# Where two sets of transfers stand in a decoder kernel's DMA queue, and how far ahead the sample tokens' work is woven

## The chip, the cores and the metric

The kernel runs on one core of one Trainium2 chip. The time is the device time of one execution in microseconds; the median of several executions counts. TensorE is called PE, VectorE DVE, ScalarE ACT, GpSimd POOL and SyncE SP. SP issues most direct transfers, POOL issues all indirect ones (gathers).

## The reference, cut to what matters

One layer of a decoder step works on 256 prompt tokens and on 32 sample tokens (8 sequences, 4 new tokens each). Everything is float32.

- `proj = x @ w_in` (2048 x about 6000 columns) for all 288 tokens. Its columns feed an RWKV-7 group (a recurrence with a 64x64 state for each of 16 heads) and a sparse-attention group (16 query heads; compressed, selected and sliding-window keys, merged by gates).
- For the sample tokens the keys are old ones: 2048 cached positions in pages, and a window of 512 positions for each sequence (`state_win_kv`). One output is the new window: positions 4 to 511 of the old one, followed by the 4 new rows. The first 508 rows of each of the 8 sequences are a plain copy, 508 x 512 values, 1.04 MB each, 8.3 MB in all.
- Both groups go through `w_out` (2048 x 2048), then `x1 = layer_norm(alpha * x + h)`.
- PEER mixer: `q = x1 @ peer_wq`, two top-16 choices over 128 sub-keys and a top-16 of their sums name 16 experts for each of 8 heads. For each token 128 rows of `peer_u` are fetched and multiplied with `x1` (the "dots"), then 128 rows of `peer_v` are summed. A second layer norm ends it.

## The kernel before, in words

The program is written as Python generators, each a stream of steps that yields a number of units now and then. `weave` (built on `woven`) draws from several streams: it always takes the next step of the stream whose drawn units, divided by the weight given for it, are lowest. A pair `(late, 137), (steps, 54)` so goes through 137 units of the one while the other goes through 54. A list scheduler then orders every engine's instructions: a step written earlier has priority over one written later, and an instruction is placed when it is ready by the scheduler's own cost model. On each engine the order is fixed from then on. `tc.issue_after(ins)` asks that the instructions in its block stand behind `ins`; it makes an order edge only for instructions on the same engine as `ins`, and no semaphore wait.

The stages that the change touches, with their times in the profile:

1. Start, 0 to 50 us. x is loaded and transposed into `XH`, `XL` (16 columns' blocks); constants, `shA` (the shift state) and small rows are loaded. Then `proj` begins: `product` loads a weight block into one of four `wraw` buffers (L390), ACT casts it to `wh` (L393), DVE or POOL makes the rest `wl` (L395), and PE runs three float32r matmuls for each block of 128 rows (L400). The first loads wait for `shA`'s transposes, whose memory they take.
2. RWKV columns, to about 320 us; then the attention columns (`proj_n`) woven with the prompt's recurrence (`prompt_steps`), to about 585 us. `proj_n` begins with eight products for the queries (`QT`, L474), each with eight loads of 128 KB, and behind each it writes one of the eight window copies, DRAM to DRAM (L477), in a block `issue_after(end.ins)`; `end` is an ACT instruction, the copy is SP's.
3. Sample attention, 585 to 800 us. `sample_late` goes through 40 units of keys (`keys`, `scored`, `applied`); each takes 1 MB of old keys and values into `co` buffers, by POOL's gathers (L434) or, for the window, by SP's loads (L877). Woven with it is the sample tokens' recurrence: `sample_states` loads the states in two halves into one buffer `big` (L1196, PE transposes L1200), `sample_steps` runs the steps (L1215 to L1312) and stores the new states (L1293). The two together yield 53.1 units, `sample_late` 137. `heads` ends each pair of sequences; `ends[bp]` keeps its PE transpose (L975).
4. From 800 us: `sample_chain` (out projection, layer norm, `peer_wq` product, choice of experts, dots of the sample tokens) woven with `prompt_attention` and `out_first` (the prompt's gates and the RWKV half of its out projection). The chain yields 69 units: 35 lie ahead of the choice, 2 are the choice, and the last 32 are the dots, two gathers (L434) and two DVE multiplications with a sum (L1517) in each. Its weights go through five `cw` buffers of 512 KB. Here the first 38 units of the chain are drawn, with weight 38, beside 19 and 19.
5. Stage "out", then "ln1": the rest of the chain is woven with `out_part(8, YN)`, the attention half of the prompt's out projection (L1625 loads, L1633 matmuls), followed by the prompt's layer norm. The prompt's x rows, 2 MB, wait in `X1` from the load at L1610 on, whose block is `issue_after(ends[2].ins)`; L1639 and L1641 add into them. The next stage, "wq", begins with L1771 (loads) and L1773 (matmuls).

The rest of the program, from "wq" on (the prompt's PEER work), is not touched.

Of the kernel before, what the change touches and what calls it, by code (L numbers as in the profile page):

```python
# [14 lines left out]
AF = mybir.ActivationFunctionType  # L15
# [3 lines left out]
P = 128  # L19

D = 2048
NT = 288
# [23 lines left out]
NR1 = 23  # L46
NP1 = 8
NDW = 1
NPRI = 12
ND = 1  # L50
NDN = 4
# [95 lines left out]
def hybrid_decode_step(ctx: ExitStack, tc: tile.TileContext, a, outs, dbg=None):  # L147
    nc = tc.nc
    ve, sc, pe, gp, sy = nc.vector, nc.scalar, nc.tensor, nc.gpsimd, nc.sync
# [58 lines left out]
    def seq(*gens):  # L208
        for g in gens:
            yield from g  # L210

    def weave(*streams):
        for _ in woven(*streams):
            pass
# [8 lines left out]
    def M_(name):  # L223
        if dbg is not None and "mark" in dbg:
            dbg["mark"](name)
# [24 lines left out]
    ident = C0("ident")  # L250
# [7 lines left out]
    QT = nq([P, 2, 4, NT], "QT")  # L258
    KT = nq([P, 2, 2, NT], "KT")
    YN = QT.rearrange("p k g t -> p (k g) t")  # L260
# [64 lines left out]
    pb = bank()  # L325
# [23 lines left out]
    for k in range(16):  # L349
        pb = bank(("p0", "p1")[k % 2])  # L350
# [5 lines left out]
    for hf in range(2):  # L356
        pb = bank()
# [22 lines left out]
    last = [None, None]  # L380
# [42 lines left out]
    pb = bank()  # L423
# [4 lines left out]
    pb = bank()  # L428
# [40 lines left out]
    def proj_n():  # L469
        for kp in range(2):  # L470
            for g in range(4):
                c0 = 3360 + 512 * kp + 64 * g
                pb = proj((c0, c0 + 64), (c0 + 256, c0 + 320))
                end = sc.activation(QT[:, kp, g, :], pb[:, :NT], AF.Copy, scale=0.125)  # L474
                b = 4 * kp + g
                with tc.issue_after(end.ins):
                    sy.dma_start(outs[9][0, b, 0:508].rearrange("t a h d -> t (a h d)"),  # L477
                                 a["state_win_kv"][0, b, 4:512].rearrange("t a h d -> t (a h d)"))
                yield 1
        for ty in (2, 3, 4, 5, None, 0, 1):  # L480
            if ty is None:
                yield from new_keys()
                continue
            dst = KT[:, ty // 2 - 1] if ty in (2, 4) else KVT[:, (0, 1, None, 2, None, 3)[ty]]
            for kp in range(2):
                c0 = 4384 + 256 * ty + 128 * kp
                pb = proj((c0, c0 + 128))
                sc.copy(dst[:, kp, :], pb[:, :NT])
                yield 1
# [94 lines left out]
    def new_keys():  # L584
        yield from kv_rows(((2, 1), (2, 2)))
        for br in range(2):
            gp.tensor_copy(KN[:, br], KT[:, br, :, NPR:])
# [263 lines left out]
    def take(gen, n):  # L851

        while n > 0:
            try:
                n_ = next(gen) or 1
            except StopIteration:
                return
            n -= n_
            yield n_


    tiles, ends = {}, {}
# [4 lines left out]
    def load(i):  # L867

        br, bp, ck = units[i]
        tiles[i] = []  # L870
        for b2 in range(2):
            pool, n_ = rings[nload[0] % len(rings)]
            nload[0] += 1
            t_ = pool([P, 1024], "co", bufs=n_)
            if br == "w":
                src = a["state_win_kv"][0, 2 * bp + b2, 256 * ck:256 * ck + 256]
                sy.dma_start(t_, src.rearrange("(p e) a h d -> p (e a h d)", e=2))  # L877
            else:
                gather(t_, rows_s, sidx[:, 2 * bp + b2, ck:ck + 1])
            tiles[i].append(t_.rearrange("p (e c) -> p e c", e=2))  # L880

    def sample_attention(sp):
# [84 lines left out]
        def heads(bp):  # L967

            x_ = sp([P, 64], "ox")
            od = sp([P, 2, 64], "od")  # L970
            ve.tensor_scalar(x_, Oa[:, bp, :64], C4("emask")[:, 0:1], None, op0=OP.mult)
            for r in range(2):
                ve.scalar_tensor_tensor(od[:, r, :], Oa[:, bp, 64:], C4("emask")[:, 1:2], x_, op0=OP.mult, op1=OP.add)
            pb = bank("st")
            ends[bp] = pe.transpose(pb[:, :P], od.rearrange("p r d -> p (r d)"), ident)  # L975
            for half in range(2):
                for b2 in range(2):
                    src = pb[hs[half], 64 * b2:64 * b2 + 64].rearrange("p (k gh gl i) -> p k gh gl i", k=4, gh=2, gl=2)[:, :, :, half, :]
                    dst = YNs[hs[half], :, 2 * bp + b2::8].rearrange("p (k gh) i -> p k gh i", k=4)
                    ve.tensor_copy(dst, src)  # L980
# [199 lines left out]
    def sample_states(sp):  # L1180

        nonlocal S0T, sPQ, sD, sBC, sUV
        S0T, sS = sp([P, 8, 8, 64], "S0T"), sp([P, 8, 232], "sS")
        sPQ = sS[:, :, 0:64].rearrange("p j (q t) -> p q j t", q=2)
        sD = sS[:, :, 64:104]
        sBC = sS[:, :, 104:168].rearrange("p j (y t) -> p j y t", y=2)
        sUV = sS[:, :, 168:232].rearrange("p j (y t) -> p j y t", y=2)
        sy.dma_start(sS[:, :, :200], RS[:, :, :])
        srw = a["state_rwkv"][0].rearrange("b (j2 jp h) v k -> b jp h v j2 k", jp=2, h=2)
        for b in range(8):  # L1190
            if b % 4 == 0:
                S0 = sp([P, 4, 4, P], "big", bufs=1)
                for b_ in range(4):
                    for jp in range(2):
                        for h in range(2):
                            sy.dma_start(S0[hs[jp], b_, :, 64 * h:64 * h + 64], srw[b + b_, jp, h])  # L1196
                yield 4 if b else 6
            pb = bank("ss")
            for j2 in range(4):
                pe.transpose(pb[:, 128 * j2:128 * j2 + 128], S0[:, b % 4, j2, :], ident)  # L1200
            sc.copy(S0T[:, b].rearrange("p j v -> p (j v)"), pb)
            yield 0.5
# [354 lines left out]
    late = sample_late(sp)  # L1557
    co = Pool("co", "right")
    rings += [(co, NCX)] * NCX
    sx = Pool("sx", "right")  # L1560
    weave((late, 137), (seq(sample_states(sx), sample_steps(sx)), 54))
    sp.close()
    nb.close()
    na.close()
# [41 lines left out]

    for t in range(2):
        for h in range(2):
            with tc.issue_after(ends[2].ins):
                sy.dma_start(X1[t][h], a["x_prompt"][0, t * P:(t + 1) * P, 1024 * h:1024 * h + 1024])  # L1610

    def out_part(o, src):
# [51 lines left out]
        yield from out_part(0, BV)  # L1664

    chain = sample_chain(cx[0])
    weave((take(chain, 38), 38), (prompt_attention(), 19), (out_first(), 19))
    M_("out")
    fewer_banks(1)
    more_banks(pa=6)  # L1670
    weave((chain, 32), (out_part(8, YN), 16))
    rw.close()
    bp_.close()
    xq = Pool("xq", "right")
# [9 lines left out]
    for t in range(2):  # L1684
# [4 lines left out]
        for q in range(4):  # L1689
            pb = bank("pa")  # L1690
# [73 lines left out]
    for h in range(9):  # L1764
        S = []
        for c in (2 * h, 2 * h + 1):
            if c < 16:
                pb = bank("pj")
# [8 lines left out]
        if h:  # L1777
# [4 lines left out]
            with tc.issue_after(chosen.ins):  # L1782
                for t, hit in enumerate(late_):
                    settle(t, h - 2, kc, hit)
                if h > 2:
                    dot(NDW, 16 * (h - 1), ahead=2)
    for t, hit in enumerate(hits):
# [13 lines left out]
    def dense(i1):  # L1801
# [4 lines left out]
        for q in range(2):  # L1806
# [3 lines left out]
            wh, wl = dp([P, 4, P], "uh", F32R, bufs=2), dp([P, 4, P], "ul", F32R, bufs=2)  # L1810
            with tc.high_priority(offset=120 + 45 * i1 if i1 < NPRI else 0):
                lo_ = columns(pb.rearrange("p (k t) -> p k t", k=4), wh, wl)
# [7 lines left out]
    for i1 in range(P):  # L1820
        lo_, mm, end = dense(i1)
# [118 lines left out]
    pb = bank("pb")  # L1940
# [141 lines left out]
```

## Time and profile before

| | us |
|---|---|
| median of 3 runs | 2633.25 (2631.76 to 2633.62) |
| the profiled execution's own time | 2648.82 |
| its span in the profile | 2647.0 |
| 0 to 50: PE busy | 16.02 |
| 585 to 640: PE busy | 40.15 |
| 640 to 760: PE busy | 117.23 |
| 800 to 1010: PE busy | 200.62 |
| 1010 to 1175: PE busy | 85.89 |
| 1175 to the end: PE busy, of 1472 | 1356.93 |

The profiled execution is slower than the median by 0.6%; its span is 1.8 us shorter than its own time. A row of busy time says how much of a stretch an engine worked; what the stretch waits for is read from the chain of waits and from the idle time of the engines. All times below count from the start of the span.

### The profile page before, as it was taken

The page shows a single profiled execution, that of the slowest core. Times are in us where ns is not written, and L with a number is a line of the kernel's source. Part 1 is how long each engine was busy: PE and PEld are TensorE (multiplying, and loading weights), DVE is VectorE, ACT ScalarE, POOL GpSimd, SP SyncE. Part 2 cuts the span into 40 slices and gives each one's busy share as a digit, 9 for nine tenths or more (in the row PEclk, how much of TensorE's full clock was granted, in tenths as well). Part 3 has the DMA queues.
Part 4 walks back from the last instruction along what each step waited for, and adds up shares of the span by engine and source line. Part 5 has one row for each costly group of instructions (what it writes and reads, how often), then busy time and mean ns, then how long its engine had stood idle before and what let it go on. Part 6 is the DMA issues. An engine that isn't in the chain of part 4 may idle for free.

```text
span 2647.0 us, 47757 instructions
## 1 busy us (share of the span) xinstructions
PE 2341.8 (88%) x17612; PEld 1963.9 (74%) x17612; DVE 1956.2 (74%) x4372; ACT 1028.9 (39%) x1938; POOL 1285.2 (49%) x1324
## 2 busy tenths in 40 slices
PE   4888999888998997649889999997689799989996
PEld 3777899875555565438789999996667588878885
DVE  2689867564753346967988888889976689888988
ACT  2333323214442243221134444444466544444443
POOL 2578523232530004745544444445556477767772
PEclk9999999988895897869999999998799899999998
DMA  8677766447664885886499999997768599998894
GB/s 254 192 235 242 217 146 183 127 141 233 223 220 154 291 273 170 317 291 184 127 338 366 343 349 350 349 350 241 227 228 297 195 338 325 323 345 322 322 324 174
DMA packets 346650, 683.49 MB, mean 258 GB/s; under 512 B 81338, under 2 KB 204785, under 8 KB 345361
## 3 DMA queue, kind: packets, MB, share of 16 engines
q1 hardware_dynamic: 251505, 344.67, 40.4%
q0 software_dynamic: 94912, 335.77, 36.2%
q8 instruction: 139, 2.28, 0.3%
q14 instruction: 94, 0.77, 0.1%
HBM read 664.77 MB, written 23.88 MB: 260 GB/s over the span
## 4 chain that ended last, share of the span: by engine, by line
PE 65%; DVE 14%; DMA 10%; issue 4%; POOL 4%; ACT 2%; SPq 1%; DVEq 0%; ACTq 0%; POOLq 0%
PE pb L2007 19%; PE ph L1815 13%; PE pj L400 6%; PE pt L1809 4%; DMA co<-in_cache_cmp_kv,gidx 2%; PE pj L1773 2%; PE pa L1633 2%; DVE rows L1739 2%; PE pa L1889 1%; PE ss L1461 1%; PE p L1044 1%; PE px L1859 1%; PE fs L1907 1%; PE sa L901 1%; DMA wraw<-in_w_in 1%
## 5 line engine op out<-in xcount | busy, mean ns | idle before, releaser
L434 POOL DMA_INDIRECT rq<-in_peer_v,gi x256 | 376.3, 1470 | 170.8 <-issue 93.3
L434 POOL DMA_INDIRECT rows<-in_peer_u,gi x256 | 299.5, 1170 | 313.7 <-DVE rows L1739 283.3
L1815 PE MATMUL ph<-XHd,ul 128*128 128x256 f32 x1024 | 304.6, 297 | 18.3 <-DVE ul L1605 18.3
L1739 DVE SCALAR_TENSOR_TENSOR rows<-rows,x1a 128x1024 f32<-128x1024 f32 x256 | 309.4, 1232 | 7.2 <-DMA rows<-in_peer_u,gi 7.2
L1815 PE MATMUL ph<-XHd,uh 128*128 128x256 f32 x1024 | 297.3, 290 | 0.3 <-ACT uh L1604 0.3
L1815 PE MATMUL ph<-XLd,uh 128*128 128x256 f32 x1024 | 290.6, 284 | 0.0
L1604 ACT CAST uh<-pt 128x512 fp32r<-128x512 f32 x256 | 149.8, 587 | 278.7 <-PE ph L1815 249.1
L400 PE MATMUL pj<-XH,wl 128*128 128x288 f32 (+1 forms) x752 | 232.9, 310 | 17.2 <-DVE wl L395 9.2
L400 PE MATMUL pj<-XH,wh 128*128 128x288 f32 (+1 forms) x752 | 230.1, 306 | 12.1 <-DVE ss L733 7.1
L1605 DVE TENSOR_TENSOR ul<-pt,uh 128x512 fp32r<-128x512 f32 x256 | 176.0, 689 | 80.5 <-ACT uh L1604 77.5
L400 PE MATMUL pj<-XL,wh 128*128 128x288 f32 (+1 forms) x752 | 226.9, 302 | 0.0
L2007 PE MATMUL pb<-vl,ah 128*128 128x512 f32 x768 | 217.3, 392 | 0.0
L393 ACT CAST wh<-wraw 128x512 fp32r<-128x512 f32 (+1 forms) x188 | 114.7, 616 | 261.8 <-PE pj L400 179.0
L2007 PE MATMUL pb<-vh,al 128*128 128x512 f32 x768 | 216.3, 390 | 0.0
L2007 PE MATMUL pb<-vh,ah 128*128 128x512 f32 x768 | 197.6, 393 | 19.6 <-ACT vh L2000 19.6
L1815 PEld LDWEIGHTS ph<-XHd,ul 128*128 128x128 f32 x1024 | 196.6, 192 | 20.6 <-DVE ul L1605 20.4
L1815 PEld LDWEIGHTS ph<-XHd,uh 128*128 128x128 f32 x1024 | 197.3, 193 | 0.9 <-ACT uh L1604 0.5
L1815 PEld LDWEIGHTS ph<-XLd,uh 128*128 128x128 f32 x1024 | 196.9, 192 | 0.0
L1981 DVE SCALAR_TENSOR_TENSOR fP<-rq,ge,fP 128x512 f32<-128x512 f32 x254 | 189.7, 747 | 4.4 <-DMA rq<-in_peer_v,gi 2.1
L2007 PEld LDWEIGHTS pb<-vh,ah 128*128 128x128 f32 x768 | 145.6, 190 | 50.5 <-ACT vh L2000 20.3
L457 DVE SCALAR_TENSOR_TENSOR CA<-co,wbc,CA 128x256 f32<-128x256 f32 x248 | 129.9, 560 | 63.9 <-DMA co<-in_cache_cmp_kv,gidx 63.7
L2007 PEld LDWEIGHTS pb<-vl,ah 128*128 128x128 f32 x768 | 145.5, 189 | 30.4
(848 smaller groups left out, 5565.3 us busy)
## 6 DMA issues: line engine op xcount, KB each, us to landing
ur<-in_peer_u SPq DMA_DIRECT2D x128, 512.0 KB
wraw<-in_w_in SPq DMA_DIRECT2D x152, 256.0 KB
cw<-in_w_out SPq DMA_DIRECT2D x32, 512.0 KB
wraw<-in_w_out SPq DMA_DIRECT2D x32, 512.0 KB
cw<-in_peer_wq SPq DMA_DIRECT2D x32, 512.0 KB
wraw<-in_peer_wq SPq DMA_DIRECT2D x32, 512.0 KB
wraw<-in_w_in SPq DMA_DIRECT2D x64, 128.0 KB
co<-in_state_win_kv SPq DMA_DIRECT2D x16, 512.0 KB
```

The costliest lines, as they stand in the source:

```text
L393: sc.copy(wh[:, :, :n], w[:, :, :n])
L400: pe.matmul(pb[:n, :nt], wi[:, k, :n], xi[(o + k) // 8][:, (o + k) % 8, :nt], start=(o + k == 0 and wi is wh and xi is xh), stop=(o + k == ...
L434: gp.indirect_dma_start(out=dst, out_offset=None, in_=rows_, in_offset=bass.IndirectOffsetOnAxis(ap=ix, axis=0))
L457: ve.scalar_tensor_tensor(d_, x_, w_, d_, op0=OP.mult, op1=OP.add)
L1604: sc.copy(xh, pb)
L1605: return ve.tensor_tensor(xl, pb, xh.bitcast(F32), OP.subtract)
L1633: pe.matmul(acc[t], xi[:, e, P * t:P * t + P], wi[:, e, :], start=(k == e == n_ == 0), stop=(k == 6 and e == 1 and n_ == 2))
L1739: i_ = ve.scalar_tensor_tensor(r_, r_, 1.0, X1a[t], op0=OP.mult, op1=OP.mult, accum_out=h_)
L1809: pe.transpose(pb[:, 128 * e:128 * e + 128], w[:, 512 * q + 128 * e:512 * q + 128 * e + 128], ident)
L1815: mm = pe.matmul(ph[:, :NPR], wi[:, e, :], xi[:, 4 * q + e, :NPR], start=(q == 0 and e == 0 and wi is wh and xi is XHd), stop=(q == 1 and ...
L1981: ve.scalar_tensor_tensor(fP[t], r_, w_, fP[t], op0=OP.mult, op1=OP.add)
L2007: pe.matmul(acc[3 * t + q], wi[:, P * t:P * t + P], xi[:, 512 * q:512 * q + 512], start=(k == 0 and wi is ah and xi is vh), stop=(k == P - ...
```

## The change

Four edits. The window copies stand behind the last weight load of their product (an SP instruction) in place of an ACT instruction. The loads of the prompt's x rows stand behind the last window load of the last pair of sequences (SP) in place of a PE transpose of the third pair. The sample tokens' recurrence is woven with weight 75 in place of 54. The chain is drawn for 52 units with weight 67.6 in place of 38 with weight 38; the rest of it has weight 18 in place of 32 beside the 16 of `out_part`.

```diff
+NCH = 52
...
-                end = sc.activation(QT[:, kp, g, :], pb[:, :NT], AF.Copy, scale=0.125)
+                sc.activation(QT[:, kp, g, :], pb[:, :NT], AF.Copy, scale=0.125)
                 b = 4 * kp + g
-                with tc.issue_after(end.ins):
+                with tc.issue_after(last[0].ins):
                     sy.dma_start(outs[9][0, b, 0:508].rearrange("t a h d -> t (a h d)"),
                                  a["state_win_kv"][0, b, 4:512].rearrange("t a h d -> t (a h d)"))
...
-                sy.dma_start(t_, src.rearrange("(p e) a h d -> p (e a h d)", e=2))
+                ends[bp] = sy.dma_start(t_, src.rearrange("(p e) a h d -> p (e a h d)", e=2))
...
-            ends[bp] = pe.transpose(pb[:, :P], od.rearrange("p r d -> p (r d)"), ident)
+            pe.transpose(pb[:, :P], od.rearrange("p r d -> p (r d)"), ident)
...
-    weave((late, 137), (seq(sample_states(sx), sample_steps(sx)), 54))
+    weave((late, 137), (seq(sample_states(sx), sample_steps(sx)), 75))
...
-            with tc.issue_after(ends[2].ins):
+            with tc.issue_after(ends[3].ins):
                 sy.dma_start(X1[t][h], a["x_prompt"][0, t * P:(t + 1) * P, 1024 * h:1024 * h + 1024])
...
-    weave((take(chain, 38), 38), (prompt_attention(), 19), (out_first(), 19))
+    weave((take(chain, NCH), 1.3 * NCH), (prompt_attention(), 19), (out_first(), 19))
...
-    weave((chain, 32), (out_part(8, YN), 16))
+    weave((chain, 70 - NCH), (out_part(8, YN), 16))
```

## Rows read from the trace of the kernel before

**Rows 1.** The page's head: span, and each engine's busy time.

```profile
span 2647.0 us, 47757 instructions
PE 2341.8 (88%) x17612; PEld 1963.9 (74%) x17612; DVE 1956.2 (74%) x4372; ACT 1028.9 (39%) x1938; POOL 1285.2 (49%) x1324
```

**Rows 2.** Busy time by stretch: length, engines' busy time, granted clock, DMA.

```profile
core 0: us, PE busy (x) PEld busy (x) DVE busy (x) ACT busy (x) POOL busy (x), PEclk, DMA share, GB/s
0.00:50.00 50.00, 16.02 (x60) 9.36 (x61) 9.19 (x28) 8.56 (x20) 14.02 (x41) 1.00 0.85 266
...
585.00:640.00 55.00, 40.15 (x428) 26.19 (x429) 26.60 (x130) 20.64 (x61) 16.07 (x17) 0.81 0.91 276
...
760.00:800.00 40.00, 30.92 (x355) 18.04 (x353) 21.85 (x90) 18.68 (x56) 7.14 (x8) 0.94 0.67 227
...
1110.00:1175.00 65.00, 12.98 (x50) 9.75 (x51) 51.92 (x102) 13.59 (x21) 39.05 (x31) 0.52 0.88 304
```

**Rows 3.** The same view, for stretches cut by the transfers.

```profile
14.00:38.00 24.00, 11.24 (x39) 5.93 (x39) 6.39 (x15) 5.28 (x14) 4.73 (x18) 1.00 1.06 343
...
340.00:400.00 60.00, 59.87 (x938) 56.54 (x936) 34.48 (x59) 15.88 (x29) 16.05 (x14) 1.00 0.59 142
833.00:1005.00 172.00, 167.38 (x1079) 100.91 (x1078) 69.87 (x211) 55.93 (x143) 9.51 (x4) 0.87 0.83 281
1005.00:1035.00 30.00, 20.67 (x140) 16.46 (x133) 21.23 (x106) 12.48 (x42) 11.34 (x21) 0.70 0.14 39
1035.00:1174.00 139.00, 69.52 (x264) 51.45 (x263) 118.13 (x195) 32.37 (x42) 94.55 (x68) 0.70 0.89 316
```

**Rows 4.** Timeline of SP's queue, 0 to 110 us.

```profile
14.19 5.57 SPq L477 DMA_DIRECT2D out<-in_state_win_kv  x8
30.49 74.83 SPq L390 DMA_DIRECT2D wraw<-in_w_in  x33
```

**Rows 5.** Line 390 between 30 and 36 us: issue times, ns min/median/max.

```profile
L390 SPq DMA_DIRECT2D wraw<-in_w_in x4: 393/896/12147, 30.5 to 32.8; - x4
```

**Rows 6.** Timeline of all engines, 0 to 62 us: two of PE's.

```profile
30.01 0.41 PE L358 MATMUL pb<-CT,shA 104*128 104x104 f32 x1 [5.17 <-DMA shA<-in_state_shift]
...
49.22 0.55 PE L400 MATMUL pj<-XH,wh 128*96 128x288 f32 x1 [4.53 <-ACT wh L393]
```

**Rows 7.** The chain that ended last, three weight loads: start, us.

```profile
30.93 17.23 DMA wraw<-in_w_in
...
329.27 5.67 DMA wraw<-in_w_in
...
503.35 3.27 DMA wraw<-in_w_in
```

**Rows 8.** Who waited for whom, 320 to 410 us: total, times, longest.

```profile
ACT wh L393 <- DMA wraw<-in_w_in: 7.7, 4, 4.0
```

**Rows 9.** Timeline of SP's queue, 585 to 900 us.

```profile
605.46 2.04 SPq L1610 DMA_DIRECT2D x<-in_x_prompt  x4
...
629.04 109.76 SPq L877 DMA_DIRECT2D co<-in_state_win_kv  x12
...
776.53 1.21 SPq L877 DMA_DIRECT2D co<-in_state_win_kv  x2
```

**Rows 10.** Timeline of PE, 575 to 645 us: waits for the states.

```profile
628.45 0.63 PE L1200 MATMUL ss<-CT,big 128*128 128x128 f32 x4 [1.77 <-DMA big<-in_state_rwkv]
...
635.40 0.63 PE L1200 MATMUL ss<-CT,big 128*128 128x128 f32 x4 [1.05 <-DMA big<-in_state_rwkv]
```

**Rows 11.** Timeline of PE, 740 to 845 us: the last of `heads`.

```profile
800.17 0.45 PE L975 MATMUL st<-CT,od 128*128 128x128 f32 x1 [2.53 <-DVE BV L1312]
```

**Rows 12.** Groups by line on DVE, 1010 to 1182 us: the dots.

```profile
L1517 DVE SCALAR_TENSOR_TENSOR cw<-cw,x 128x1024 f32<-128x1024 f32 x64 | 84.3, 1334 | 22.5 <-DMA cw<-in_peer_u,gi 12.1 <-DMA cw<-in_peer_u,ig 10.1
```

**Rows 13.** Timeline of POOL, 1018 to 1024 us: the first gather of the dots.

```profile
1023.38 1.01 POOL L434 DMA_INDIRECT cw<-in_peer_u,gi  x1 [1.72 <-DVE CV L1320]
```

**Rows 14.** Timeline of PE, 1171 to 1176 us: stage "wq" begins.

```profile
1174.31 2.08 PE L1773 MATMUL pj<-XT,wraw 128*128 128x256 f32 x4 [6.24 <-DMA wraw<-in_peer_wq]
```

## The prediction

> **What bounds the kernel now.** I read the page first, then busy time by stretch, then, for each stretch that an edit touches, the queue of the transfers concerned and the waits on PE. The page makes PE the bound at 88% of the span, with no other engine over 74% [rows 1]; but that is a mean. An edit that moves transfers and order can gain only where PE is idle, so the reader should look for PE's holes first. There are four in the stretches touched: 34 us of the first 50 (PE 16.0), 15 us of 585 to 640, 9 us of 760 to 800, and 52 us of 1110 to 1175 [rows 2]. Between 340 and 400 and between 833 and 1005 PE is nearly full, 59.9 of 60 and 167 of 172 [rows 3]: nothing moved there gains by itself, and what is put in there may cost. From 1175 us on the program is the same, and I carry its 1472 us over.
>
> **Edit 1, the window copies: where they leave.** All eight are issued from 14.2 us on [rows 4], not in the query products where they are written: `end` is an ACT instruction and the copies are SP's, so the order edge was never made. They are 8.3 MB (8 x 1.04). From 14 to 38 us the DMA engines are full (share 1.06) at 343 GB/s [rows 3], so the copies alone take 8.3 / 0.343 = 24 us of them. What is late for it: PE waits 5.17 us for `shA` before its transposes at 30.0 [rows 6]; the first weight load takes 17.2 us where later ones take 5.7 and 3.3 [rows 7], and one issue beside it holds SP for 12.1 us [rows 5]; the first product starts at 49.2 [rows 6]. Without the copies the first 5.2 us go (x's own transposes run until then, so no more), and the load shrinks by 17.2 - 5.7 = 11.5 to 17.2 - 3.3 = 13.9. Together 16.7 to 19.1. I take -17: what follows, up to 320 us, is the same chain of work and moves forward whole. The lower end for the gain is 10, if the many small rows of that first load keep it slower than the later ones.
>
> **Edit 1: where they arrive.** With an edge from SP to SP each copy goes right behind its product's loads, in the stretch of the query products, about 320 to 400 us. Each takes 24 / 8 = 3.0 us of all DMA engines, and loads of the next product queue behind it. Between 340 and 400 the DMA share is 0.59 [rows 3], so 60 x 0.41 = 25 us are free for 24 us of copies: they just fit, at PE's expense only where a load comes too late for its cast. Today casts wait 7.7 us for loads from 320 to 410, in four waits of at most 4.0 [rows 8]; PE runs through. The cost is between 0 (four buffers hold a whole product, so a load may be 3 us late) and 24 (none of it covered). I take +4, near the lower end, because PE's row is full while DMA's is not. The gathers on POOL's queue share the engines and are 3 us late at most.
>
> *Here a rule of the Trainium skill speaks against the edit.* The copies kept the DMA engines at a share of 1.06 of all sixteen over 24 us [rows 3]. The Trainium skill, page "DMA: Bandwidth & Descriptors", section "Why a DMA increments its semaphore by 16 and not by 1", says that a transfer uses the largest number of engines up to 16 that divides its slowest dimension; for 508 rows that is 4, unless software splits a contiguous run differently. By that each copy would hold four engines four times as long. The row contradicts the narrow case here; what it would cost is the fourth rival.
>
> **Edit 2, the prompt's x rows.** The same kind of edge that was not made: the four loads, 2.1 MB, are issued at 605.5 [rows 9], in the stretch where DMA has a share of 0.91 and PE idles 15 us [rows 2]. At 276 GB/s they take 7.6 us of it. What waits behind them are the second half's states: PE stands 1.77 and 1.05 us for them [rows 10]. Behind the last window load (about 776.5 to 777.7, [rows 9]) they meet a share of 0.67 [rows 2], and their first reader (L1639) stands in the stage that begins at 800, behind the first quarter of `out_first`'s products, so this end is free. Between 0 and -7.6; I take -3, the two waits.
>
> **Edit 3, recurrence at 75.** It removes and adds no instruction. It ends after 53.1 / 75 = 71% of `sample_late`'s units, not 97%. Between 640 and 760 PE is full, so there the order is all that changes. The gain is at the end: PE's last transpose waits 2.53 us for the recurrence's last additions [rows 11], and 760 to 800 has 9 us of idle PE [rows 2]. What comes late next: the last 11 or so key units run without filler from the recurrence. Each takes 1 MB, 1.05 / 0.276 = 3.8 us at the rate of 585 to 640, so 11 of them take 42 us against the 40 us of the tail now. Bounds: -9 (all the idle time) to +8 (PE stops more often there, and its clock falls as in 585 to 640, granted 0.81 [rows 2]). I take -3, the wait of [rows 11].
>
> **Edit 4, the chain.** 52 - 38 = 14 more of its steps are drawn beside attention, all of them dots: 28 gathers of 512 KB and 28 DVE multiplications of 1.33 us [rows 12]. Also, the first 38 are drawn 1.78 times as fast against attention. Now, the first gather is issued at 1023.4 [rows 13], after a stretch (1005 to 1035) in which DMA moves only 39 GB/s [rows 3], because the choice of experts needs no transfers and nothing else has any left. After it, to 1174, DMA runs at 316 GB/s and DVE at 118 of 139 us while PE works 69.5 [rows 3]: the dots set the pace there, and stage "wq" starts only at 1174.3, after 6.2 us of waiting for its weights [rows 14] behind the last gathers. With the dots begun earlier, 28 x 1.33 = 37 us of DVE, or 28 x 0.524 / 0.316 = 46 us of DMA, leave this stretch. They go where DVE is at 70 of 172 us and DMA at 0.83 [rows 3]: room for 172 x 0.17 = 29 us of DMA. So of the 37 at most 29 are truly won; none, if attention is put back by as much as the chain is put forward, for PE is full there. I take -20, two thirds of 29, since the idle 30 us at 39 GB/s are filled by loads of attention's partner `out_first`, but the choice itself still takes its time.
>
> **Sum.** -17 + 4 - 3 - 3 - 20 = -39 us on the profiled execution's 2648.8 (span 2647.0 [rows 1] and 1.8 around it): 2610. The median shown lies 0.6% below that execution, so 2594 for the median, -1.5%.
>
> **The rivals.** *Nothing from the chain.* The moved dots take DMA that the 64 weight loads of the chain need, and the stretch before 1005 grows by what the one behind loses: 167 of 172 us of PE speaks for it, the hole of 30 us against. -17 + 4 - 6 = -19: 2614. *Order edge without effect.* If a block behind an SP transfer gets no edge either, copies and x rows stay at 14 and 605 us and only edits 3 and 4 act: about -23, 2610; the trace of before has no such pair to judge by. *Dots in attention's way (slower).* Place: DVE, in the last third of the stretch with attention. Each dot stands 1.33 us in front of attention's own steps on DVE; if all 28 do, attention and with it the second half of the out projection and the layer norm end 37 us later, and nothing is won behind: -17 + 4 - 6 + 37 = +18, 2651. It decides against the change once 18 of the 28 stand in the way (18 x 1.33 = 24, against 19 gained elsewhere, plus the 5 that can be told apart). DVE's 70 of 172 us speaks against. *Copies on few engines (slower).* A copy would take 12 us in place of 3, eight of them 97; the 25 us free cover a quarter: +72 in place of +4, so -17 + 72 - 26 = +29, 2662. The 343 GB/s of [rows 3] speaks against.
>
> **Chances and range.** Forecast 0.62; nothing from the chain 0.21; edge without effect 0.06; dots in the way 0.07; copies on few engines 0.04. A measurement of this kernel tells changes above 0.2%, 5 us, from none. Faster takes the first three, less 0.04 for values near zero: 0.85; same 0.05; slower 0.10. The range goes from 2566 (start -19, copies 0, edits 2 and 3 -12, chain -36 at nearly its DVE bound) to 2626 (start -10, copies +9, nothing from the chain, edits 2 and 3 -6): the first three cases lie in it, the two slower ones do not.
>
> **What would show it.** The first product at about 32 us, not 49. Copies on SP between 320 and 400, PE still near 60 of 60 there; more than 10 us of PE idle would make +4 wrong. The x rows behind 760 us, no wait over 1 us for the second states. The last state stores before 750. The first gather of the dots near 990 less the 19 us gained before, no stretch of 30 us under 50 GB/s behind it, and "wq" beginning about 39 us earlier than 1174. The prediction is wrong if attention's last transposes come later than now less 19 by over 10 us, or if the query products wait for loads.

## The result, and the profile after

The changed kernel takes 2646.9 us (median of 6 executions, 2640.0 to 2660.4), the kernel before 2632.3: medians 14.6 us apart. The ratio is 1.0069, 95% interval 1.0049 to 1.0088. It is slower by 0.7%, where 1.5% faster was predicted. Timed once more beside the experiments, it came to 1.0069 again (1.0044 to 1.0094).

Lines of the changed kernel have numbers one above those of before. The page's head, against [rows 1]:

```profile
span 2643.3 us, 47762 instructions
...
PE 2339.4 (89%) x17612; PEld 1967.9 (74%) x17612; DVE 1950.9 (74%) x4372; ACT 1028.0 (39%) x1938; POOL 1285.9 (49%) x1324
```

By this pair of profiles alone the change would have gained 3.7 us of span. But the profiled execution of before was an unusually long one: another took 2632.0 us and has a span of 2630.3. Busy time by stretch of the kernel after, columns as in [rows 2]:

```profile
0.00:50.00 50.00, 34.49 (x179) 27.60 (x180) 18.09 (x44) 16.36 (x37) 21.94 (x51) 1.00 0.65 182
340.00:400.00 60.00, 58.24 (x817) 54.64 (x814) 33.50 (x66) 16.57 (x29) 13.26 (x12) 0.97 0.76 223
1005.00:1035.00 30.00, 21.89 (x127) 16.64 (x126) 21.44 (x89) 11.27 (x25) 8.86 (x17) 0.72 0.06 19
...
1110.00:1175.00 65.00, 26.84 (x96) 20.98 (x96) 46.80 (x78) 7.43 (x11) 37.16 (x35) 0.63 1.00 352
```

The start is fuller: PE 34.5 of 50 against 16.0 [rows 2]. Among the query products PE idles 1.8 us of 60, 0.1 before [rows 3]. The hole in front of the dots, 39 GB/s before [rows 3], is still there, with 19. The stretch 1110 to 1175, in which "wq" now begins, is full of transfers, 352 GB/s. SP's and POOL's timelines show the moved transfers, against [rows 4, 9, 13]:

```profile
310.54 0.52 SPq L478 DMA_DIRECT2D out<-in_state_win_kv  x1
...
323.20 0.53 SPq L478 DMA_DIRECT2D out<-in_state_win_kv  x1
...
768.98 1.83 SPq L1611 DMA_DIRECT2D x<-in_x_prompt  x4
```

```profile
1027.83 1.01 POOL L435 DMA_INDIRECT cw<-in_peer_u,gi  x1 [3.11 <-DVE ge L1379]
```

Both order edges act. The first gather of the dots comes at 1027.8; it was at 1023.4 in the first profile of before [rows 13] and is at 1009.3 in a second one. So the dots begin later than before, not earlier.

The landmarks of seven profiles, in us from the start of each span (starts of instructions; "ends" where it says so). "Before 2" and "after 2" are second profiles of the same kernels; the last three columns are experiments (below).

| | before | before 2 | after | after 2 | no_chain | chain_only | quarters_xrows |
|---|---|---|---|---|---|---|---|
| first product | 49.2 | 47.8 | 29.7 | 32.0 | 29.7 | 50.7 | 28.8 |
| norm transposes end (W2) | 590.0 | 589.4 | 582.5 | 581.8 | 585.9 | 587.6 | 576.4 |
| last `heads` ends | 800.6 | 794.2 | 788.6 | 801.6 | 790.1 | 791.8 | 773.8 |
| chain's first product | 838.8 | 831.2 | 825.2 | 837.0 | 825.9 | 830.0 | 810.6 |
| sample norm's product | 924.1 | 913.0 | 926.3 | 934.9 | 905.2 | 918.2 | 897.0 |
| chain's last product ends | 1005.3 | 991.1 | 1006.0 | 1014.8 | 992.9 | 1010.7 | 971.1 |
| first dot | 1028.5 | 1014.4 | 1032.2 | 1041.0 | 1018.9 | 1032.0 | 994.4 |
| last dot ends | 1180.8 | 1165.6 | 1182.6 | 1194.2 | 1171.2 | 1186.7 | 1149.8 |
| "wq" begins | 1174.3 | 1152.0 | 1146.8 | 1156.6 | 1165.8 | 1163.9 | 1110.9 |
| "wq" products end | 1293.3 | 1279.0 | 1291.6 | 1303.5 | 1285.5 | 1293.2 | 1259.2 |
| span | 2647.0 | 2630.3 | 2643.3 | 2655.8 | 2636.8 | 2645.7 | 2612.1 |

"W2" is the stage of the attention columns and the prompt's recurrence. Read against "before 2", the change is 7 to 8 us ahead at 590 us and 12 to 24 behind at the end of "wq"; the rest takes 1350 to 1354 us in all 20 profiles taken. The loss lies between 590 and 1293 us, and from the chain's last product on each column roughly keeps its distance.

One profile is one execution, and a landmark of it moves without any edit. Nine profiles of kernels with the copies at the start have the same PE order up to W2 (at most 4 of 5537 instructions stand elsewhere), and their W2 ends lie between 584.5 and 594.6 us, 590.4 in the mean. The products of the chain took 164.3 us in one profile of *copies_only* and 177.2 in the other. Differences of that size between two single profiles show nothing by themselves.

### The profile page after: what moved, and what is told of

Its sections match the earlier page's. It is cut to its first block, busy times and chain, and to the rows that moved or that the text cites. A ratio compares the mean times of both kernels' runs of the same rounds, so it can differ in the third digit from the quotient of the medians.

```text
span 2643.3 us, 47762 instructions
## 1 busy us (share of the span) xinstructions
PE 2339.4 (89%) x17612; PEld 1967.9 (74%) x17612; DVE 1950.9 (74%) x4372; ACT 1028.0 (39%) x1938; POOL 1285.9 (49%) x1324
## 4 chain that ended last, share of the span: by engine, by line
PE 67%; DVE 13%; DMA 8%; issue 5%; POOL 4%; ACT 2%; SPq 1%; DVEq 0%; POOLq 0%; ACTq 0%
PE pb L2008 19%; PE ph L1816 13%; PE pj L401 7%; PE pt L1810 4%; PE pa L1634 2%; DMA co<-in_cache_cmp_kv,gidx 2%; DVE rows L1740 2%; PE p L1045 2%; PE pa L1890 2%; PE sa L902 1%; PE pj L1774 1%; PE px L1860 1%; PE ss L1462 1%; POOL cw L435 1%; PE fs L1908 1%
## 5 line engine op out<-in xcount | busy, mean ns | idle before, releaser
L401 PEld LDWEIGHTS pj<-XH,wl 128*128 128x128 f32 (+1 forms) x752 | 146.3, 194 | 35.3 <-DVE wl L396 20.5
```

What stands on the lines that cost most here:

```text
L401: pe.matmul(pb[:n, :nt], wi[:, k, :n], xi[(o + k) // 8][:, (o + k) % 8, :nt], start=(o + k == 0 and wi is wh and xi is xh), stop=(o + k == ...
```

## The experiments

All ratios are to the kernel before on the same chip, with 95% intervals.

**One edit alone.** Four kernels, each with one of the change's edits as its diff shows it.

*copies_only* (and *copies_again*, the same kernel, for a second profile):

```diff
-                with tc.issue_after(end.ins):
+                with tc.issue_after(last[0].ins):
```

> Only the window copies are moved; the rest is the kernel before. Theory A (the chain's new order is what costs): the start gives 19 to 20 us, the copies' arrival takes 12 to 13 back by 590 us, nothing else moves, so 7 us faster than before, some 2625 us, ratio 0.997. Theory B (the copies cost more where they arrive than the start gives, and the pair of profiles hides it because the profiled execution of before was an untypically long one): ratio 1.003 to 1.006, and the last product of the attention columns ends later than that of an execution of before with the usual time.

> The kernel with the copies' edit alone once more, for the profile of another execution of it: its executions lay between 2633.8 and 2673.2 us and the profiled one was among its shortest. Theory arrival: the long ones lose their time between 320 and 550 us, PE waiting for loads. Theory clock: up to 550 us they agree within 5 us, and the difference of over 10 us lies in stretches of granted clock 0.5 behind it.

Measured 1.0057 (1.0022 to 1.0093) and 1.0038 (1.0011 to 1.0065). The first products come at 29.4 and 30.1 us, but the W2 transposes end at 588.3 and 592.4: the 18 us are gone by then. Theory A's 7 us faster falls; the ratios are those of theory B, but its sign, the attention columns' last product later than in a usual execution of before, shows in one of the two (547.3 and 551.1 us, 548.5 in "before 2"). The two profiles agree within 4.1 us up to 590 us and end 7.8 us apart, so the spread between executions of this kernel does not come from the arrival. The mean granted clock was 0.921 and 0.925 over the executions, 0.930 and 0.932 for before beside them: part of the loss goes with a lower clock behind W2. What lowers it isn't shown.

*xrows_only* (L877, L975, L1609 of the diff):

> Only the four loads of the prompt's x rows are moved behind the last window load. Both theories: within 0.1% of before; at most 3 us faster, by the two waits for the states (1.77 and 1.05 us) that it removes. A third theory, that these loads delay the chain's first weights in their new place, gives up to 7 us slower (2.1 MB at 276 GB/s).

Measured 0.9998 (0.9969 to 1.0027): no difference that can be told, as both theories said.

*rec75_only*, the weight 54 to 75:

> Only the weight of the sample tokens' recurrence goes from 54 to 75. Both theories: the recurrence ends some 25 to 30 us earlier and the stage up to 800 us is 2 to 5 us shorter; ratio 0.998 to 0.999. A theory that the units of keys are left without filler gives up to 8 us slower.

Measured 1.0057 (1.0034 to 1.0081), 15 us slower. Its recurrence ends only 4 us earlier (last addition at 790.4 us; 794.0 in "before 2"), and the last `heads` 11 us later (804.9 against 794.2), of which 3 us stand at W2 already. Both theories had the recurrence 25 to 30 us earlier and fall; 15 us is also more than the 8 of the theory of missing filler. The loss behind W2 begins behind the state transposes. Stretch 640 to 660 us of "before 2", then of rec75_only, columns as above:

```profile
640.00:660.00 20.00, 20.00 (x256) 12.84 (x256) 9.98 (x36) 6.29 (x19) 4.17 (x5) 0.83 0.42 141
```

```profile
640.00:660.00 20.00, 19.76 (x297) 16.72 (x301) 6.42 (x24) 4.13 (x12) 2.51 (x3) 0.56 0.37 133
```

and PE's groups from 636 to 660 us, again "before 2" first (count, busy time, mean ns):

```profile
L901 PE MATMUL sa<-CT,co 128*128 128x128 f32 x38 | 7.5, 328 | 0.0
L1215 PE MATMUL ss<-sS,S0T 64*64 64x8 f32 x154 | 6.8, 204 | 0.2 <-issue 0.2
```

```profile
L1215 PE MATMUL ss<-sS,S0T 64*64 64x8 f32 x224 | 11.4, 237 | 0.2 <-issue 0.2
L901 PE MATMUL sa<-CT,co 128*128 128x128 f32 x20 | 4.6, 399 | 0.0
```

PE is full in both. With 75 it does 224 products of 8 columns in place of 154, and 20 key transposes in place of 38, at a granted clock of 0.56 in place of 0.83; the first `heads` follows 9 us later (673.3 against 664.5), the second 15. Each side of this comparison is one profile.

*chain_only*:

> Only the chain's length and weights are changed (52 units at 67.6, then 18). Theory A: the prompt's attention and its out projection end 23 us earlier, but the dots don't begin earlier, and the stage with the second weights runs beside the rest of the dots' gathers and gives more back than it got: ratio 1.005 to 1.010, 13 to 26 us slower. Theory B: what is won ahead of that stage is given back and no more, ratio 0.998 to 1.002. My prediction's step had 20 us faster, ratio 0.992.

Measured 1.001 (0.9981 to 1.0039): neither theory A's size nor my 20 us; theory B's. This is the fourth edit's own result, and its interval excludes a gain over 5 us. In its profile the chain's last product ends 19.5 us later than in "before 2", with nearly the same beginning.

**All but the chain.** *no_chain* is the changed kernel with 38, 38 and 32 at the chain.

> The changed kernel without its fourth edit (the chain's length and weights). If the edits' costs measured alone add up (copies 1.006, x rows 1.000, recurrence 1.006), ratio 1.010 to 1.013. If they don't add, because each shifts the same stretches of low clock, 1.003 to 1.007, that of the whole change.

Measured 1.0024 (1.0008 to 1.0040), a little below the 1.003 to 1.007 of costs that don't add. So they don't, and the fourth edit on top makes 1.0069 of it: some 12 us (4 to 20, with this interval and that of *after_again* taken as independent). Alone it cost 3 us (-5 to 10), so that it costs more in company is likely and not certain.

**A profile each.** *before_again* is the kernel before, *after_again* the changed one.

> The kernel before once more, for a profile of an execution with the usual time: the profiled one took 2648.8 us, the 64 executions of it timed beside the experiments 2616 to 2653, in the mean 2630 and 2639. Theory: up to the last norm transposes (590 us) and from the last product of the second weights (1293 us) to the end it agrees with the profile of before within 3 us; between them it needs some 690 us, not 703, with fewer stretches of granted clock 0.5 between 640 and 1110. Rival: the usual execution is shorter evenly, 1% in all stages.

> The changed kernel once more, on the chip of the experiments. If its loss is real: ratio 1.004 to 1.009 as before; the stretch from the last norm transposes to the last product of the second weights takes 705 to 712 us (709 in the first profile). If the first result was an accident of the chip: ratio 0.996 to 1.002.

*before_again* took 2632.0 us and needs 689.6 us from the W2 transposes to the end of "wq" (before: 703.3), and begins that stage within 1 us of it: 13.7 of the 16.7 us by which the profiled execution was longer lay in that stage. *after_again* measured 1.0069 and needs 721.7 us there, more than the 705 to 712 expected (709.0 in the first profile): the loss is real and repeats, its size in a profile does not.

**Where the copies go.** *copies_out* leaves them out (that output's first 508 rows are not written). *copies_keys* puts each behind one of the first eight key and value products. *copies_tail* puts all eight behind the last load of the peer_v table:

```diff
+            if k + 4 == P:
+                with tc.issue_after(raw[-1].ins):
+                    for b in range(8):
+                        sy.dma_start(outs[9][0, b, 0:508]...
```

*copies_quarters* cuts each into four, one behind each pair of loads of the query products:

```diff
+                if parts and c1 == n:
+                    b, r = divmod(parts.pop(0), 4)
+                    with tc.issue_after(last[0].ins):
+                        sy.dma_start(outs[9][0, b, 127 * r:127 * r + 127]...
```

> The kernel before without the eight window copies (the first 508 rows of that output are not written). Alone, moving the copies made it slower by 0.2 to 0.9% although the first product began 19.8 us earlier; its executions had a granted clock of 0.921 in the mean, those of before 0.930. Theory arrival (the copies hold up the loads of the query products): without them the whole gain of the start stays, 15 to 20 us faster, ratio 0.992 to 0.994. Theory clock (the earlier start and the order the scheduler makes from it lose the gain in granted clock later, copies or not): ratio 1.000 to 1.006, granted clock 0.92 to 0.925.

> The copies stand one stage later, each behind the last load of one of the first eight products of the keys and values, some 400 to 520 us, where the DMA share of before is 0.50. Theory arrival: there is room for them there, so 12 to 20 us faster than before, ratio 0.992 to 0.995. Theory clock: ratio 1.000 to 1.006.

> The eight copies behind the last load of the peer_v table, some 2594 us, where the DMA share is 0.70 for 10 us and then 0.00 to 0.01 up to the last stores at 2621; nothing else is changed. Theory arrival: as without the copies, 5 to 10 us faster than before, ratio 0.996 to 0.998, 15 us or more faster than with the copies among the query products. Rival: they hold up the last gathers and the last stores, by as much as their own 24 us: ratio 1.002 to 1.007.

> The copies among the query products as in the change, but each in four quarters (127 rows), one behind each pair of loads in place of a whole copy behind eight. Theory burst (a whole copy of 65,024-byte pieces stands 3 us in front of the next loads and gathers): most of the 10 to 14 us that the arrival costs goes, ratio 0.997 to 1.000. Theory room (the DMA engines have no room there for 24 us of copies): as the whole copies, ratio 1.003 to 1.006.

Without the copies: 0.9982 (0.9965 to 0.9998), W2 ends at 578.3. So their arrival costs 10 to 14 us by the two profiles of edit 1 alone (588.3, 592.4), 8 in the mean of the five profiles that have them behind the query products in the same PE order, and 22 among the key products (600.5; ratio 1.008, 1.0058 to 1.0101), where theory arrival had a gain: a low mean DMA share did not say that there was room. But 11 of the start's 18 to 20 us is all that is left at 590 even without copies, and of those the ratio shows 5, where theory arrival had 15 to 20. At the tail: 0.9983 (0.9949 to 1.0017): undecided. In quarters: 0.9955 (0.9930 to 0.9980), W2 ends at 577.2 (576.4 and 577.0 in the two kernels further down that have them too): theory burst. Stretch 340 to 400 of copies_again; the first row of its PE waits from 300 to 460 us (total, times, longest); the stretch in copies_quarters:

```profile
340.00:400.00 60.00, 56.73 (x815) 53.19 (x814) 30.82 (x57) 15.61 (x28) 9.98 (x10) 0.97 0.75 208
```

```profile
PE pj L400 <- DVE wl L395: 6.0, 3, 3.3
```

```profile
340.00:400.00 60.00, 59.84 (x849) 56.04 (x849) 35.62 (x71) 17.08 (x31) 12.98 (x12) 1.00 0.77 213
```

The same bytes and the same share, but PE stays full when no load stands behind a whole copy.

**How fast the chain is drawn.** Only the numbers at the chain's `weave` differ from the kernel before: *chain38_fast* 38 units at 49.4, *chain52_even* 52 at 52, *chain38_slow* 38 at 28.5, *chain38_178* 38 at 67.6.

> The kernel before, with the first 38 units of the chain drawn with weight 49.4 (1.3 times as fast beside attention), no dots among them. In 13 of the profiles so far the last product of the chain ends 159 to 177 us after its first one without the fourth edit, 178 to 181 us with it, and the last product of the second weights follows 107 to 115 us behind the last dot whatever attention does. Theory rate (what costs is that the chain's narrow products are drawn faster in front of the wide products of the out projection): the chain's products take 170 to 176 us, ratio 1.001 to 1.004. Theory dots (what costs are the 14 units of dots drawn beside attention): 160 to 168 us, ratio 0.997 to 1.001.

> 52 units of the chain at weight 52: 1.37 times as fast as before (the changed kernel: 1.78 times), with the 14 units of dots. Theory rate: as the kernel with 38 units at 1.3, the chain's products 170 to 176 us, ratio 1.001 to 1.004. Theory dots: 178 to 181 us, the same as with the fourth edit alone, ratio 1.001 to 1.005, and more than with 38 units at 1.3.

> 38 units of the chain at weight 28.5: drawn 0.75 times as fast. Theory rate: the wide products come earlier, the granted clock returns earlier, and the chain's products take 150 to 160 us, ratio 0.995 to 0.999. Rival (the later draw puts the chain itself back): 170 us or more, ratio 1.003 to 1.008, with attention's last transposes 5 to 15 us earlier.

> 38 units of the chain, no dots among them, at the changed kernel's rate, weight 67.6 (1.78 times as fast as before). Neither 1.3 times without dots (the chain's products 164 us, ratio 0.998) nor 1.37 times with 14 units of dots (162 us, 0.9965) cost anything, so both earlier theories fall as they stood. Theory threshold (the rate alone, above some value between 1.37 and 1.78, makes the order that costs): the chain's products 175 to 181 us, ratio 1.000 to 1.004. Theory both (dots and rate only together): 158 to 168 us, ratio 0.996 to 1.000.

Measured 0.9980 (0.9954 to 1.0006), 0.9965 (0.9942 to 0.9988), 1.0022 (0.9997 to 1.0047) and 0.9999 (0.9975 to 1.0024); the chain's products take 163.8, 161.7, 167.1 and 168.1 us (159.9 in "before 2", 180.7 in chain_only). Neither the dots nor a moderate rate costs anything, so theories rate and dots fall as they stood. The slow draw's 167.1 us and 1.0022 lie between its theory and its rival. chain38_178 lies at theory both's edge, not in theory threshold's range. But up to the end of attention its PE order is that of chain_only, and yet the chain's products differ by 12.6 us, as much as between two profiles of one kernel (above), and the two ratios can't be told apart. So chain_only's 180.7 shows no cost of its order, and there is no cost of the fourth edit alone left to explain.

**Parts together.** *quarters_xrows* has the copies in quarters and edit 2; *best* has chain52_even's numbers as well.

> The copies in quarters behind the pairs of loads of the query products, and the x rows behind the last window load; the rest as before. The copies in quarters alone had ratio 0.9955 [0.993, 0.998], the x rows alone 0.9998 [0.997, 1.003]. If both hold and add: 0.993 to 0.998. If the x rows disturb the order of the stage behind: 0.998 to 1.002.

> The copies in quarters, the x rows behind the last window load (together 0.9942) and the chain with 52 units at weight 52 (alone 0.9965); the recurrence stays at 54. If these add: ratio 0.989 to 0.993. If the chain's gain is one of an order that the other edits change anyway: 0.993 to 0.997.

Measured 0.9942 (0.9918 to 0.9965) and 0.9938 (0.9907 to 0.9970). Both beat both kernels, the one before by at least 0.3%; the chain's numbers add nothing that can be told.

## Why the prediction was wrong

Alone, in us and by the ratios: edit 1 was forecast at -13 (-17 + 4) and measured at +10 and +15; edit 2 at -3, measured 0; edit 3 at -3, measured +15; edit 4 at -20, measured +3 with no gain over 5 us. The step on which the size of the forecast rested, edit 4's, failed, and edit 1's sum missed by as much.

**The start (-17): right in size, wrong that it "moves forward whole".** The first product came 15.7 to 19.5 us earlier. At the end of W2 11 us of that are left without copies, 7 to 8 in the changed kernel. I carried the start's gain to the end as one term. What takes the rest isn't shown.

**The copies' arrival (+4): mechanism right, size low.** In the changed kernel W2 ends 3.4 to 4.2 us behind copies_out, with the edit alone 10 and 14. Those are executions of one PE order, so they are one spread and no two costs; the five end at 586.2 us in the mean, 8 behind copies_out. The bound of 24 held. What costs is a whole copy in front of a product's loads. But +8 in place of +4 doesn't make +10 to +15 of -13: at W2 the two profiles of edit 1 alone stand where before stands, so what they lose lies behind it, where the copies have long landed.

The copies are not on few engines: each left as 16 packets of 65,024 bytes (128 for the eight), 2.4 to 4.0 us each, and the 16 of the first copy start within 1.4 us and run side by side. The Trainium skill, page "DMA: Bandwidth & Descriptors", section "Why a DMA increments its semaphore by 16 and not by 1", would have 4 engines for 508 rows and a single one for 127 unless software splits a contiguous run; the quarters, of 127 rows, also left as 16 packets each (512 of 16,256 bytes, median 0.61 us), so the trace fits its exception and not its rule; how the run was split, no row says.

**Edit 2 (-3): not measurable alone.** The loads stand at 769 us, but PE still waits for the second states, 2.57 us once in the changed kernel, and 0.95 to 2.80 in all six profiles with the edit; "before 2" has no such wait, though its x rows load at 605. So moving the x rows does not remove the waits of [rows 10]. Beside the quarters the step from 0.9955 to 0.9942 lies within both intervals.

**Edit 3 (-3): wrong sign.** I named the falling clock as a bound of +8 and put it at the end of the stage; it fell at its beginning. Alone the edit cost 15 us. In the changed kernel the recurrence did end early (last addition at 767.8 us), and still the last `heads` came 206.1 us behind W2 (219.8 in its second profile), against 204.8 in "before 2" and 210.6 in before. So ending the recurrence earlier won nothing there: the wait of [rows 11] was not a gain to be had.

**Edit 4 (-20): the step that failed.** "With the dots begun earlier" was the step: 37 us of dots would leave the stretch in front of "wq", and -20 of that be won. The dots did not begin earlier. Counted from the chain's first product the first dot comes 207.0 and 204.0 us behind in the changed kernel, 202.0 in chain_only; in the twelve profiles with the chain's old numbers it comes 183 to 193 us behind, once 205. The prediction named the reason as its own exception: PE is full there. The changed kernel's static order has more work, not less, in front of the chain's next steps. From the chain's first product to the sample norm, "before 2", no_chain and after:

```profile
831.20:913.00 81.80, 81.34 (x489) 45.69 (x489) 32.67 (x92) 23.19 (x55) 4.74 (x2) 0.85 0.92 317
```

```profile
825.90:905.20 79.30, 78.29 (x500) 44.65 (x500) 33.55 (x103) 25.64 (x65) 4.74 (x2) 0.89 0.97 335
```

```profile
825.20:926.30 101.10, 100.91 (x565) 60.33 (x564) 36.65 (x116) 29.27 (x79) 6.56 (x3) 0.76 0.78 267
```

PE idles 0.2 to 1.0 us in each. The same stretches by PE's groups, "before 2", then after:

```profile
L1633 PE MATMUL pa<-wh,YH 128*128 128x512 f32 x40 | 16.9, 423 | 0.0
...
L1461 PE MATMUL ss<-cw,YNs 128*32 128x256 f32 x128 | 13.3, 513 | 0.0
...
L693 PE MATMUL sao<-vs,PTs 128*128 128x64 f32 x16 | 3.8, 323 | 0.0
```

```profile
L1634 PE MATMUL pa<-wh,YH 128*128 128x512 f32 x44 | 19.6, 445 | 0.0
...
L1462 PE MATMUL ss<-cw,YNs 128*32 128x256 f32 x128 | 13.5, 513 | 0.0
...
L694 PE MATMUL sao<-vs,PTs 128*128 128x64 f32 x24 | 5.8, 331 | 0.0
...
L630 PE MATMUL sa<-cb,QT 64*128 64x8 f32 x32 | 4.2, 255 | 0.0
```

The chain's 128 products of this group take 13.3 and 13.5 us. What grew is the rest: 44 out projection products of each kind in place of 40, and up to half as much again of attention's. But this count is not the cause of the loss, and it is not edit 4's own. xrows_only and quarters_xrows, both with the chain's old numbers and one PE order between them up to the end of attention, have 561 instructions there:

```profile
828.30:921.50 93.20, 91.68 (x561) 54.27 (x561) 37.61 (x116) 28.89 (x78) 7.10 (x3) 0.83 0.85 291
```

```profile
810.60:897.00 86.40, 84.06 (x561) 50.83 (x561) 37.49 (x116) 28.90 (x78) 7.10 (x3) 0.92 0.91 314
```

The one has the ratio 0.9998, the other 0.9942. At the same count the stretch is shorter where the granted clock is higher: 101.1 us at 0.76 (after; 97.9 in its second profile), 93.2 at 0.83, 86.4 at 0.92. If quarters_xrows is taken as the measure, about 7 us over no_chain's 79.3 go with the 60 to 65 instructions more, and about 15 with the clock; that is an estimate from single profiles. *best* needs 97.0 us there and is still among the fastest. So what is shown is that the dots come later and that edit 4 gains nothing alone; why the whole change loses 18 us, why its clock stays low longer, and why the combination gives this order, stays open.

**What sets the end: missed.** I read that the dots set the pace in front of "wq", and let the 1472 us behind 1175 move with the beginning of "wq". It does not. DVE's sum over the dots and the prompt's first choice of experts, and ACT's steps between them, in "before 2" and after:

```profile
1165.59 0.19 DVE L1519 TENSOR_TENSOR hd<-hd 128x32 f32<-128x32 f32 x1
...
1183.88 0.49 DVE L1318 MAX8 HV<-TB 128x8 f32<-128x128 f32 x2 [17.61 <-ACT TB L1338]
```

```profile
1165.82 0.23 ACT L1520 ACTIVATE hd<-hd 128x32 f32<-128x32 f32 x1 [27.38 <-DVE hd L1519]
1166.43 2.05 ACT L1392 COPY SKT<-pb 128x512 f32<-128x512 f32 x4 [0.38 <-DMA wraw<-in_peer_wq]
```

```profile
1182.62 0.19 DVE L1520 TENSOR_TENSOR hd<-hd 128x32 f32<-128x32 f32 x1
...
1196.41 0.49 DVE L1319 MAX8 HV<-TB 128x8 f32<-128x128 f32 x2 [13.11 <-ACT TB L1339]
```

```profile
1182.85 0.23 ACT L1521 ACTIVATE hd<-hd 128x32 f32<-128x32 f32 x1 [53.90 <-DVE hd L1520]
1183.46 2.05 ACT L1393 COPY SKT<-pb 128x512 f32<-128x512 f32 x4 [0.38 <-DVE ge L1522]
```

ACT's Gelu (L1520, L1521 after) needs the last dot, and in ACT's fixed order it stands in front of the copies of the sub-keys (`SKT`) and of all the products of "wq" (`QP`), in all 20 profiles. ACT waits for it, 27.38 and 53.90 us here, and PE waits for ACT's copies of `QP`, 14.3 us once in the changed kernel. So an early start of "wq" ends in a longer wait: in all 20 profiles its products end 106 to 115 us behind the last dot, whether it began at 1111 or at 1174; the dots themselves take 144 to 155 us in all. So the time behind 800 us is the chain's: its products, the choice, the dots, the prompt's choice. No run moves that Gelu; whether "wq" would gain by it stays untested. That attention, the out projection and the layer norm ended 9 us earlier than in "before 2", and "wq" began 5 us earlier, was worth nothing.

**The rivals.** "Nothing from the chain" had the nearest reason, but at -19 in all. "Dots in attention's way" had nearly the time, 2651, by luck; its mechanism fell: attention's last transposes ended at 1024.8 and 1033.7 us, 1033.9 in "before 2"; what came later was the chain itself. "Order edge without effect" and "copies on few engines" did not occur.

**The signs named.** The first product, the copies (their packets run from 287 to 380 us, the first ones earlier than the 320 named; PE idles 1.8 us, not over 10) and the x rows came as said. The wait for the second states (2.57 us, not under 1), the last state stores (762 us), the first gather (1027.8), the hole at 19 GB/s and the beginning of "wq" (27 us earlier than in before, 5 earlier than in "before 2", where 39 were named) did not. One figure of the working was off without effect: 53.1 units at 54 end after 98% of the other stream's, not 97.

## What to carry to other kernels

Before an edge or a weight is moved, find which stream's last step the next stage really waits for, and price only what moves that step; a hole in PE beside it is not a gain. Look too at what stands behind that step on every engine: here one small ACT instruction held up the copies behind it. Where PE is full, a higher weight for one stream rearranges what stands in front of it; counting instructions ahead of a step did not tell the outcome here (561 in the fastest kernel, 565 in the changed one), so measure the order. Spread a large copy between loads in pieces, and take a second profile of the kernel before when the profiled execution differs from the median by as much as the effect sought: profiles of one order here differed by 10 us and more at a landmark.

## What was not expected of the hardware

Executions of one kernel differ by more than the edits do, and mostly with the granted clock: 35 executions of before, timed beside copies_only, took 2618 to 2653 us, and the twelve of copies_only 2634 us at a mean granted clock of 0.926 to 2673 at 0.911. Between those twelve the time rises by 2.1 us where the mean clock falls by 0.001 (correlation -0.97; before's 35: 1.7 and -0.73). A granted clock near 0.5, the level of 1.2 GHz, holds long just behind 800 us, with PE busy 16 to 20 us of each 20; "before 2" and after, 800 to 820 and 840 to 860:

```profile
800.00:820.00 20.00, 17.22 (x75) 13.06 (x76) 4.68 (x21) 0.83 (x3) 0.00 (x0) 0.53 0.12 27
840.00:860.00 20.00, 20.00 (x90) 9.28 (x92) 6.62 (x11) 4.00 (x7) 0.00 (x0) 0.59 0.80 267
```

```profile
800.00:820.00 20.00, 16.07 (x77) 11.29 (x76) 6.34 (x33) 4.83 (x21) 0.00 (x0) 0.59 0.14 37
840.00:860.00 20.00, 20.00 (x78) 9.18 (x76) 7.09 (x22) 4.05 (x13) 0.00 (x0) 0.50 0.57 194
```

A kernel can so begin earlier and end later: copies_only had a mean granted clock of 0.921 over its executions, before 0.930. That the clock goes with the time is shown; what makes it fall in one execution and not in another is not.
